# One level of seven block products for the output projections of two row tiles

## The chip, the cores and the metric

The kernel runs on one core of a Trainium2 chip. The metric is the device time of one execution in microseconds; the figure for a kernel is the median of its runs.

## What is computed

One decoder layer on 2048 rows of 1024 channels, in float32:

```python
hn = rms_norm(h, mix_pre_g)
proj = hn @ w_in                                   # q, k, v and the convolution's input u
attn_out = sliding_window_attention(q, k, v, attn_sinks, rel_bias)
conv_out = conformer_conv(u, conv_dw, conv_dw_b, conv_ln_g, conv_ln_b, w_conv_pw)
mixed = jnp.concatenate([attn_out, conv_out], axis=-1) @ w_out
h = h + rms_norm(mixed, mix_post_g)
hn = rms_norm(h, ffn_pre_g)
ff = (jax.nn.silu(hn @ w_gate) * (hn @ w_up)) @ w_down
h = h + rms_norm(ff, ffn_post_g)
```

The change concerns the line with `w_out`: 512 attention channels and 512 convolution channels times a 1024 x 1024 matrix. `w_join` is the convolution's pointwise matrix, multiplied beforehand into the lower half of `w_out`.

## The kernel before

**Tiles and precision.** The rows are cut into four tiles of 512 (numbered 0 to 3 in the code; "tiles 3 and 4" of the text are numbers 2 and 3). Each float32 operand is split into a high part (a rounded copy, made by ACT) and a low part (the rest, made by DVE), and a product takes three matmuls of 128x128 by 128x512: high by high, high by low, low by high.

**Stages.** The label behind the `@` in a tile's name tells the stage: `A` input projection, `B` attention, `C` convolution, `W` output projection and the norms behind it, `H` operands of the feed-forward, `F` gate and up projections, `G` down projection. The feed-forward works on two tiles at a time (first 0 and 1, then 2 and 3) and already uses one level of seven block products; its order for a pair is `stage_pre` (products that need the first tile of the pair alone), `stage_p1` and `stage_p2` (the down projection).

**Lanes.** The program is written out in one order. A main generator is run, and at each of its yields (a number, a nominal time) several lanes are pumped, each with its own rate, so that their instructions are emitted among the main ones. Instructions emitted earlier have priority; a compile-time pass then fixes the order on each engine, and each engine works strictly through its own. During `stage_p2` of the first pair (77 steps of 4 yields of 0.69), lane `lw` runs at rate 1.25 and holds the output projections of tiles 2 and 3.

**An output projection (`stage_w`).** For tiles 2 and 3 the four attention chunks are loaded from `mixT`, the four convolution chunks come from `stage_tail` within the same generator. Four steps of two chunks by two halves of the output: the weights are loaded (`raw`), their low parts are reloaded from `lo_out`, where the first tile's projection stored them, and `block_half` multiplies them for four row blocks in rotating PSUM banks `tr` and adds each result to `acc` (`mid@W`). The convolution's channels are needed only from the third step on. `norm_w` then makes the mean square, scales by the gains (`gb`), adds `x`, stores `h_scr`, norms again and stores `hn_scr`.

**What follows.** `stage_h_plain` reloads `hn_scr`, turns it on PE and makes the operands `B11` (tile `ql@H` in this pair) and `B21` (`mid@H`), each of four chunks, through tiles `gb`. `stage_pre` of the second pair begins with two products on `B11`, then two on `B21`. `B11.2` is queued in `lw`; `B21.2` in another lane, once the norm of tile 3 is emitted. `stage_h_sums` needs tile 3 too.

**Buffers.** Tiles of one name share a fixed count of buffers; those named below: `gb` 2, `ql` 4, `chl` 5, `mid` 4, `at` 2, `fc` 3, `yt` 1, `raw` 2, `w` 6. In PSUM: `mm` 4 banks, `tr` 3, `ct` 1.

**Taps.** The convolution of tiles 2 and 3 runs on DVE in lane `lc` (tile `y2`), ends in stores to `y_scr`, and `stage_tail` starts from there: load, turn on PE (L614), statistics, rsqrt, normalise, turn back (L667), swish.

Of the kernel before, what the change touches and what calls it, by code (L numbers as in the profile page):

```python
# [12 lines left out]
F32 = mybir.dt.float32  # L13
# [4 lines left out]
AF = mybir.ActivationFunctionType  # L18
ALU = mybir.AluOpType
# [4 lines left out]
D = 1024  # L24
DFF = 2816
P = 128
T = 512
NT = S // T
KC = D // P
# [8 lines left out]
def layer_kernel(ctx, tc, x, xT, cols, rows, sinks, relb, onehot, w_in, w_four, w_pw, w_out, w_gate, w_up, w_down, out):  # L38
    nc = tc.nc
# [61 lines left out]
    vtt = dve(nc.vector.tensor_tensor)  # L101
# [5 lines left out]
    def mat(*args, **kw):  # L107
        r = nc.tensor.matmul(*args, **kw)  # L108
        if not inlane[0]:
            lead_pe[0] = r  # L110
        return r
# [498 lines left out]
    def turner(yt, ycs):  # L610
        def turn(c):
            b = ct()
            for s in range(4):
                nc.tensor.transpose(b[:, s * P : (s + 1) * P], ycs[c][:, s * P : (s + 1) * P], ident)  # L614
            act(yt[:, :, c * P : (c + 1) * P], b.rearrange("p (s c) -> p s c", c=P), AF.Copy)

        return turn
# [16 lines left out]
    def stage_tail(t, sink=None):  # L634
        L = f"C{t}"
        lab[0] = L
        yt = t_("yt", (P, 4, 4 * P))
        ycs = []
        turn = turner(yt, ycs)
        for c in range(4):  # L640
            lab[0] = L
            y = f2("fc")
            nc.sync.dma_start(y, y_scr[c, :, t * T : (t + 1) * T])
            ycs.append(y)
            turn(c)
            yield 0.5
        yield from conv_tail(t, yt, sink)
# [111 lines left out]
    def ss(s):  # L759
        return slice((s % 4) * P, (s % 4 + 1) * P)  # L760
# [27 lines left out]
    def stage_w(w, spill, G, atag, htag, mtag, bank_of, norm=None):  # L788
        L = f"W{w}"
        lab[0] = L  # L790
        acc = [f4(atag) for _ in range(4)]

        def operand(m):
            a = hl(htag)
            act(a[:, 0], m, AF.Copy)
            vtt(a[:, 1], m, a[:, 0].bitcast(F32), ALU.subtract)
            return [a]

        def acts(gi, ms=None):
            return [operand(m) for m in ms or load(gi)]  # L800

        conv = []
        tail = stage_tail(w, lambda v: conv.append(operand(v))) if w > 1 else ()
        for y in tail:
            if y == YL2:
                break
            yield y
        lab[0] = L

        stage = spare_tile() if w == 1 else None  # L810

        def load(gi):
            ms = []
            pair_ = stage if w == 1 else t_("chl", (P, 2, T)) if w else t_("wx", (P, 2, T)) if gi == 0 else None
# [6 lines left out]
        gb = load_gb(0) if w > 1 else None  # L821
        if w != 1:
            yield 5.0 if w == 0 else 8.0
            lab[0] = L
        nxt = acts(0, first)
        for gi in range(KC // G):
            if w > 1 and G * gi == 4:
                yield from tail
                lab[0] = L
            aa = nxt if w < 2 or G * gi < 4 else conv[G * gi - 4 : G * gi - 4 + G]  # L830
            for n in range(2):
                lab[0] = L
                more = gi + 1 < KC // G and (w < 2 or G * gi + G < 4)
                if n == 0 and more:
                    if w < 2 and G * gi + G == 4:
# [9 lines left out]
        last = norm_w(w, spill, acc, mtag, gb)  # L845
        if norm:
            norm(last)
        else:
            yield from last

    def norm_w(w, spill, acc, mtag, gb):
# [12 lines left out]
        for s in range(4):  # L864
            lab[0] = L
            post_scale(acc[s], gb, r[:, s : s + 1])
            r0 = w * T + s * P
            if s == (2 if mtag == "fa" else 0):
                xt = f4("wx")
                nc.sync.dma_start(xt, x[r0 : r0 + P])  # L870
                vtt(acc[s], xt, acc[s], ALU.add)
            else:
                for n in range(2):
                    cs = slice(n * T, (n + 1) * T)
                    xt = f2(mtag if s == 1 or w > 1 else "fa")
                    nc.sync.dma_start(xt, x[r0 : r0 + P, cs])
                    vtt(acc[s][:, cs], xt, acc[s][:, cs], ALU.add)
            nc.sync.dma_start(h_scr[r0 : r0 + P], acc[s])
            act(junk, acc[s], AF.Square, accum_out=ssq2[:, s : s + 1])
            yield 5.0  # L880
        lab[0] = L
        r2 = rsqrt(ssq2, 4, D, False)
        yield 3
        lab[0] = L
        for s in range(4):
            act(acc[s], acc[s], AF.Copy, scale=r2[:, s : s + 1])
        if spill:
            yield 2.0
            lab[0] = L
            for s in range(4):  # L890
                r0 = w * T + s * P
                nc.sync.dma_start(hn_scr[r0 : r0 + P], acc[s])
        yield 0.1
        hns[w] = acc
# [8 lines left out]
    def split_f(x, w):  # L903
        act(w[:, 0], x, AF.Copy)  # L904
# [497 lines left out]
    def since(lane, name, dt):  # L1402
        return name in lane.done and clk[0] >= lane.done[name] + dt
# [51 lines left out]
    RC0, RC1, RC2, RC3, RW0, RW, RB, LC = 0.7, 1.1, 0.35, 0.9, 1.7, 1.25, 0.8, 100  # L1455
# [3 lines left out]
    CS = 10  # L1459
    YC = 3  # L1460
    YP = 1.5
    YL, YL2 = 12, 20
# [12 lines left out]
    lc = Lane(RC0, LC)  # L1475
    lw = Lane(RW0, 0)
# [7 lines left out]
    lw.rates = {"W0": RW0, "C2": RW, "W2": RW, "C3": RW, "W3": RW}  # L1484

    def run(gen):
        for c in gen:
# [65 lines left out]
    ws, ops = (0, 1), {}  # L1553
    for n, off in (("B11", 0), ("B21", 4)):
# [85 lines left out]
```

## Time and profile before

| | us |
|---|---|
| median of 3 runs | 1907.33 |
| lowest, highest | 1906.63, 1907.36 |
| span of the profiled execution | 1907.9 |
| PE busy | 1889.1 |
| DVE busy | 1490.7 |
| ACT busy | 970.6 |
| first matmul of the first pair's down projection | 950.8 |
| first matmul of the second pair's feed-forward | 1265.5 |

The page gives no time of the profiled execution beside its span; the span is 0.6 us above the median. PE is TensorE, DVE VectorE, ACT ScalarE, POOL GpSimd, SP SyncE; SPq and ACTq are DMA issues by SP and ACT. A row of a group reads: line, engine, operation, output<-inputs, shapes, count | busy us, mean ns of one | idle us before it and what ended that. A row of a window reads: its bounds and length, then busy us and instructions of PE, weight loads, DVE, ACT and POOL (of one tile's instructions alone where the window is of a tile, with the engines that it has), PE's granted clock, the DMA engines' busy share and GB/s. A row of the timeline reads: start, length, engine, line, operation, count and, in brackets, the idle time before. A row of the chain of waits reads: start, length, what.

### The profile page before, as it was taken

The page shows a single profiled execution, that of the slowest core. Times are in us where ns is not written, and L with a number is a line of the kernel's source. Part 1 is how long each engine was busy: PE and PEld are TensorE (multiplying, and loading weights), DVE is VectorE, ACT ScalarE, POOL GpSimd, SP SyncE. Part 2 cuts the span into 40 slices and gives each one's busy share as a digit, 9 for nine tenths or more (in the row PEclk, how much of TensorE's full clock was granted, in tenths as well). Part 3 has the DMA queues.
Part 4 walks back from the last instruction along what each step waited for, and adds up shares of the span by engine and source line. Part 5 has one row for each costly group of instructions (what it writes and reads, how often), then busy time and mean ns, then how long its engine had stood idle before and what let it go on. Part 6 is the DMA issues. An engine that isn't in the chain of part 4 may idle for free.

```text
span 1907.9 us, 26569 instructions
## 1 busy us (share of the span) xinstructions
PE 1889.1 (99%) x8714; PEld 1530.1 (80%) x8714; DVE 1490.7 (78%) x2721; ACT 970.6 (51%) x1912; POOL 179.2 (9%) x196
## 2 busy tenths in 40 slices
PE   9999999999999999999999999999999999999998
PEld 8777777777777888888888878788888888888886
DVE  6999999987966999999996765887567674455558
ACT  5356445566667433433445574685443433345452
POOL 2010001110000000000000000010033233211002
PEclk9999999999999999999999999999999999999999
DMA  9887746679688677877776596798554443375663
GB/s 353 300 281 238 248 160 207 230 228 318 218 274 276 232 234 232 293 261 243 244 268 195 196 326 212 259 333 307 166 176 156 160 138 127 116 258 187 206 220 133
DMA packets 226491, 439.29 MB, mean 230 GB/s; under 512 B 22536, under 2 KB 48560, under 8 KB 226352
## 3 DMA queue, kind: packets, MB, share of 16 engines
q1 hardware_dynamic: 207344, 411.37, 64.8%
q10 hardware_dynamic: 17088, 19.93, 2.9%
q0 software_dynamic: 1920, 6.29, 0.9%
q8 instruction: 68, 1.11, 0.2%
q14 instruction: 71, 0.58, 0.1%
HBM read 318.48 MB, written 119.02 MB: 229 GB/s over the span
## 4 chain that ended last, share of the span: by engine, by line
PE 78%; DVE 9%; DMA 8%; ACT 3%; issue 2%; SPq 0%; ACTq 0%; DVEq 0%; POOL 0%; POOLq 0%
PE mm@F L108 34%; PE mm@G L108 16%; PE mm@A L108 14%; PE tr@W L108 5%; PE mm@W L108 3%; PE tr@B L108 2%; PE ct@J L108 1%; DVE w@F L85 1%; DVE mid@W L85 1%; DMA hl@A<-x 1%; DVE sm@G L85 1%; DVE y2@C L85 1%; DMA chl@H<-hT 1%; DVE hl@G L85 1%; DMA chl@F<-w_gate 1%
## 5 line engine op out<-in xcount | busy, mean ns | idle before, releaser
L108 PE MATMUL mm@F<-hl@H,w@F 128*128 128x512 f32 x1056 | 255.8, 391 | 1.8 <-ACT mm@F L1058 1.6
L108 PEld LDWEIGHTS mm@F<-hl@H,w@F 128*128 128x128 f32 x1056 | 197.7, 188 | 44.8 <-ACT mm@F L1058 2.8
L108 PE MATMUL mm@G<-hl@G,hl@G 128*128 128x512 f32 x924 | 226.1, 393 | 2.3 <-ACT hl@G L904 1.5
L904 ACT ACTIVATE w@F<-chl@F 128x512 fp32r<-128x512 f32 x220 | 136.5, 626 | 170.2 <-PE mm@F L108 158.7
L108 PEld LDWEIGHTS mm@G<-hl@G,hl@G 128*128 128x128 f32 x924 | 171.5, 188 | 39.7 <-ACT hl@G L904 2.2
L108 PE MATMUL mm@G<-w@G,hl@G 128*128 128x512 f32 x876 | 199.8, 389 | 0.6 <-DVE w@G L85 0.6
L108 PEld LDWEIGHTS mm@G<-w@G,hl@G 128*128 128x128 f32 x876 | 164.3, 188 | 35.2 <-DVE w@G L85 1.0
L108 PE MATMUL mm@A<-hl@A,w@A 128*128 128x512 f32 x792 | 192.2, 394 | 0.0
L108 PEld LDWEIGHTS mm@A<-hl@A,w@A 128*128 128x128 f32 x792 | 146.8, 188 | 32.5 <-issue 1.7
L85 DVE TENSOR_TENSOR w@F<-chl@F,w@F 128x512 fp32r<-128x512 f32 x198 | 148.1, 753 | 25.5 <-ACT w@F L904 25.0
L85 DVE SCALAR_TENSOR_TENSOR y2@C<-g2@C,colt,y2@C 128x1024 f32<-128x1024 f32 x120 | 154.0, 1283 | 0.2
L108 PE MATMUL mm@F<-mid@H,w@F 128*128 128x512 f32 x528 | 130.6, 390 | 1.0 <-DVE w@F L85 0.9
L108 PE MATMUL mm@F<-ql@H,w@F 128*128 128x512 f32 x528 | 129.7, 390 | 0.2
L108 PE MATMUL mm@F<-p@H,w@F 128*128 128x512 f32 x528 | 129.1, 389 | 0.0
L108 PE MATMUL mm@F<-x@H,w@F 128*128 128x512 f32 x528 | 127.8, 390 | 0.0
L108 PEld LDWEIGHTS mm@F<-mid@H,w@F 128*128 128x128 f32 x528 | 98.8, 188 | 22.2 <-DVE w@F L85 1.3
L108 PEld LDWEIGHTS mm@F<-ql@H,w@F 128*128 128x128 f32 x528 | 98.7, 188 | 21.3 <-DVE w@F L85 0.6
L108 PEld LDWEIGHTS mm@F<-x@H,w@F 128*128 128x128 f32 x528 | 98.7, 188 | 21.3 <-issue 0.8
L108 PEld LDWEIGHTS mm@F<-p@H,w@F 128*128 128x128 f32 x528 | 99.1, 188 | 20.6
L133 ACT ACTIVATE w@A<-raw@A 128x512 fp32r<-128x512 f32 x100 | 60.9, 625 | 80.2 <-PE mm@A L108 46.3
L85 DVE TENSOR_TENSOR w@G<-raw@G,w@G 128x512 fp32r<-128x512 f32 x72 | 50.2, 698 | 64.2 <-ACT w@G L904 63.4
L108 PE MATMUL mm@W<-w@W,hl@W 128*128 128x512 f32 x384 | 97.1, 399 | 0.8 <-DVE x@W L85 0.4
(322 smaller groups left out, 3363.9 us busy)
## 6 DMA issues: line engine op xcount, KB each, us to landing
mids<-fa@F SPq DMA_DIRECT2D x154, 256.0 KB, 3.3
raw@A<-w_in SPq DMA_DIRECT2D x50, 512.0 KB, 4.9
w@A<-lo_in SPq DMA_DIRECT2D x84, 256.0 KB, 4.0
fa@G<-mids SPq DMA_DIRECT2D x74, 256.0 KB, 4.7
fc@G<-mids SPq DMA_DIRECT2D x72, 256.0 KB, 3.5
w@W<-lo_out SPq DMA_DIRECT2D x48, 256.0 KB, 4.8
chl@F<-w_gate SPq DMA_DIRECT2D x22, 512.0 KB, 4.4
raw@F<-w_gate SPq DMA_DIRECT2D x22, 512.0 KB, 4.2
```

The costliest lines, as they stand in the source:

```text
L85: r = op(*args, **kw)
L108: r = nc.tensor.matmul(*args, **kw)
L133: act(w[:, 0], raw, AF.Copy)
L904: act(w[:, 0], x, AF.Copy)
```

## The change

The projections of tiles 2 and 3 are taken out of `stage_w` and made together by one level of seven block products: the two tiles and the two halves of the channels (attention, convolution) form 2 x 2 blocks on the left, the two halves of the channels and of the outputs 2 x 2 blocks of the weights. `stage_vsums` makes four sums of row blocks and four of weight blocks and stores them in DRAM (`vs0`, `vs1`). `stage_v` makes the seven kinds in turn, each over four chunks and in four PSUM banks held throughout (`tr` three times, `ct`), with results kept in the two tiles' `acc` (`mid` and `chl`). It loads all its operands, splits both sides itself and no longer reads `lo_out`. `stage_tail` of both tiles now stores its channels to `mixT`. Lane `lw` holds, in this order: both tails, the sums, the products, both norms (with one pair of gain tiles), `B11.2`. The loop of `stage_w` remains for tiles 0 and 1.

```diff
@@ stage_w
-        conv = []
-        tail = stage_tail(w, lambda v: conv.append(operand(v))) if w > 1 else ()
-        for y in tail:
-            if y == YL2:
-                break
-            yield y
...
+    def stage_vsums(ws, ma, mb_):
+        L = f"W{ws[0]}"
+        cols_ = [slice(w * T, (w + 1) * T) for w in ws]
+
+        def load(c):
+            lab[0] = L
+            a = [t_("chl", (P, 2, T)) for _ in range(2)]
+            b = [t_("raw", (P, 2, T)) for _ in range(2)]
+            for j in range(2):
+                nc.sync.dma_start(b[j], (w_join if j else w_out)[c].rearrange("p (a b) -> p a b", a=2))
+                nc.sync.dma_start(a[j], mixT[c::4, :, cols_[j]].rearrange("j p t -> p j t"))
+            return a, b
+
+        yield 6.0
+        nxt = load(0)
+        yield 6.0
+        for c in range(4):
+            a, b = nxt
+            (a11, a12), (a21, a22) = [(t[:, 0], t[:, 1]) for t in a]
+            (b11, b12), (b21, b22) = [(t[:, 0], t[:, 1]) for t in b]
+            for to, o, p_, op, q_, dst in (
+                (0, b11, b12, ALU.subtract, b11, mb_), (2, b12, b22, ALU.subtract, b12, mb_),
+                (1, b22, b22, ALU.subtract, b11, mb_), (3, b21, b21, ALU.subtract, b22, mb_),
+                (2, a22, a21, ALU.add, a22, ma), (1, a21, a11, ALU.subtract, a21, ma),
+                (0, a11, a22, ALU.subtract, a11, ma), (3, a12, a12, ALU.subtract, a11, ma)):
+                lab[0] = L
+                vtt(o, p_, q_, op)
+                nc.sync.dma_start(dst[to, c], o)
+                yield 0.8
+            if c < 3:
+                nxt = load(c + 1)
+                yield 2.0
+
+    def stage_v(ws, ma, mb_, accs, gbs):
+        L = f"W{ws[0]}"
+        lab[0] = L
+        banks = [tr(), tr(), tr(), ct()]
+        for acc, tag in zip(accs, ("mid", "chl")):
+            acc += [f4(tag) for _ in range(4)]
...
+        stage = t_("yt", (P, 2, 2, T))
+        steps = [(ty, c) for ty in range(7) for c in range(4)]
...
+        def load(h):
+            if 2 * h < len(steps):
+                lab[0] = L
+                rb = t_("raw", (P, 2, T))
+                nc.sync.dma_start(rb, right(*steps[2 * h]).rearrange("j p t -> p j t"))
+                ra = stage[:, h % 2]
+                nc.sync.dma_start(ra, left(*steps[2 * h]).rearrange("j p t -> p j t"))
...
+        def split(i):
+            if i < len(steps):
+                lab[0] = L
+                b = split_f(rawb[i], hl("w"))
+                lo(rawb.pop(i), b, False)
+                a = split_f(rawa[i], hl("ql"))
+                lo(rawa.pop(i), a, False)
+                opsd[i] = a, b
+
+        def after(ty, b):
...
+            if ty == 0:
+                act(u1, o, AF.Copy)
+            elif ty == 1:
+                nc.vector.tensor_copy(c11, o)
+                act(o, u1, AF.Copy)
+            elif ty == 2:
+                act(u2, o, AF.Copy)
+            elif ty == 3:
+                vtt(c22, o, u2, ALU.subtract)
+            elif ty == 4:
+                nc.vector.tensor_copy(c21, o)
+                act(o, u2, AF.Copy)
+            elif ty == 5:
+                vtt(c22, c22, o, ALU.add)
+            else:
+                act(c12, o, AF.Copy)
...
+        for i, (ty, c) in enumerate(steps):
+            split(i + 3)
+            if i % 2 == 0:
+                load(i // 2 + 3)
...
+            for b in range(4):
...
+                for z, (p_, q_) in enumerate(((ah, w[:, 0]), (ah, w[:, 1]), (al, w[:, 0]))):
+                    mat(banks[b], p_, q_, start=i == 0 and z == 0, stop=c == 3 and z == 2, skip_group_check=True)
+                if c == 3:
+                    after(ty, b)
+                yield 0.69
...
@@ the order
-    lw.add("W2", stage_w(2, True, 2, "mid", "ql", "at", tr), lambda: since(lc, "T2", CS))
-    lw.add("W3", stage_w(3, True, 2, "mid", "ql", "at", tr, norm=lambda g: lw.add("N3", g)),
-           lambda: since(lc, "T2", CS))
+    for w in ws:
+        lw.add(f"C{w}", stage_tail(w), lambda: since(lc, "T2", CS))
+    vs = [dr.tile([4, 4, P, T], F32, name=f"vs{i}") for i in range(2)]
+    accs, gbv = ([], []), []
+    lw.add("WS", stage_vsums(ws, *vs))
+    lw.add("V", stage_v(ws, *vs, accs, gbv))
+    for w in ws:
+        lw.add(f"N{w}", norm_w(w, True, accs[w - 2], "at", gbv))
     lw.add("B11.2", stage_h_plain(ws, ops, "B11", 0))
```

More of the change, by code (lines that the diff above doesn't have):

```diff
@@ L813, in load @@
             ms = []
-            pair_ = stage if w == 1 else t_("chl", (P, 2, T)) if w else t_("wx", (P, 2, T)) if gi == 0 else None
+            pair_ = stage if w else t_("wx", (P, 2, T)) if gi == 0 else None
             for c in range(G * gi, G * gi + G):
@@ L820, in stage_w @@
         first = load(0)
-        gb = load_gb(0) if w > 1 else None
-        if w != 1:
-            yield 5.0 if w == 0 else 8.0
+        if w == 0:
+            yield 5.0
             lab[0] = L
@@ L826, in stage_w @@
         for gi in range(KC // G):
[L827 to L830, printed above, removed]
+            aa = nxt
             for n in range(2):
                 lab[0] = L
-                more = gi + 1 < KC // G and (w < 2 or G * gi + G < 4)
+                more = gi + 1 < KC // G
                 if n == 0 and more:
-                    if w < 2 and G * gi + G == 4:
+                    if G * gi + G == 4:
                         ld.until(f"C{w}")
@@ L844, in stage_w @@
                 yield from block_half(acc, list(zip(aa, ws)), n, gi == 0, L, bank_of)
-        last = norm_w(w, spill, acc, mtag, gb)
+        last = norm_w(w, spill, acc, mtag)
         if norm:
@@ L849, in stage_w @@
             yield from last
-    def norm_w(w, spill, acc, mtag, gb):
+    def stage_vsums(ws, ma, mb_):
[28 more added lines that the diff above has]
+                yield 2.0
@@ new lines, in stage_v, with left, right @@
+    def stage_v(ws, ma, mb_, accs, gbs):
[4 more added lines that the diff above has]
+            acc += [f4(tag) for _ in range(4)]
+        n0, n1 = slice(0, T), slice(T, D)
+        cols_ = [slice(w * T, (w + 1) * T) for w in ws]
+        stage = t_("yt", (P, 2, 2, T))
+        steps = [(ty, c) for ty in range(7) for c in range(4)]
+        rawa, rawb, opsd = {}, {}, {}
+        def left(ty, c):
+            if ty < 2:
+                return mixT[4 * ty + c : 4 * ty + c + 2, :, cols_[0]]
+            if ty == 4:
+                return mixT[4 + c : 6 + c, :, cols_[1]]
+            return ma[{2: 0, 3: 1, 5: 2, 6: 3}[ty], c : c + 2]
+        def right(ty, c):
+            if ty in (0, 1, 6):
+                return (w_join if ty else w_out)[c : c + 2, :, n1 if ty == 6 else n0]
+            return mb_[{2: 1, 3: 2, 4: 3, 5: 0}[ty], c : c + 2]
+        def load(h):
[5 more added lines that the diff above has]
+                nc.sync.dma_start(ra, left(*steps[2 * h]).rearrange("j p t -> p j t"))
+                for j in range(2):
+                    rawa[2 * h + j], rawb[2 * h + j] = ra[:, j], rb[:, j]
+        def split(i):
[7 more added lines that the diff above has]
+        def after(ty, b):
+            lab[0] = L
+            o = banks[b]
+            (c11, c12), (c21, c22) = [(acc[b][:, n0], acc[b][:, n1]) for acc in accs]
+            u1, u2 = c21, c12
+            if ty == 0:
[14 more added lines that the diff above has]
+                act(c12, o, AF.Copy)
+        load(0)
+        load(1)
+        yield 8.0
+        for i in range(3):
+            split(i)
+        load(2)
+        yield 2.0
+        for i, (ty, c) in enumerate(steps):
+            split(i + 3)
+            if i % 2 == 0:
+                load(i // 2 + 3)
+            if i == len(steps) - 4:
+                lab[0] = L
+                gbs += load_gb(0)
+            for b in range(4):
+                lab[0] = L
+                (a, w) = opsd[i]
+                ah, al = a[:, 0, ss(b)], a[:, 1, ss(b)]
+                for z, (p_, q_) in enumerate(((ah, w[:, 0]), (ah, w[:, 1]), (al, w[:, 0]))):
[3 more added lines that the diff above has]
+                yield 0.69
+            del opsd[i]
@@ L852, in norm_w @@
+    def norm_w(w, spill, acc, mtag, gb=None):
         L = f"W{w}"
@@ L1483, in layer_kernel @@
     lc.rates = {"T0": RC0, "T1": RC1, "T2": RC2}
-    lw.rates = {"W0": RW0, "C2": RW, "W2": RW, "C3": RW, "W3": RW}
+    lw.rates = {"W0": RW0, "C2": RW}
     def run(gen):
```

1 line of the change is left out of this document (removed).

## The prediction

> **What bounds the kernel now.** I read the page first, then the groups of instructions, then the chain of waits and the timelines from 930 to 1300 us, where the changed stage lies.
>
> ```profile
> span 1907.9 us, 26569 instructions
> PE 1889.1 (99%) x8714; PEld 1530.1 (80%) x8714; DVE 1490.7 (78%) x2721; ACT 970.6 (51%) x1912; POOL 179.2 (9%) x196
> ```
> ```profile
> L108 PE MATMUL mm@G<-hl@G,hl@G 128*128 128x512 f32 x924 | 226.1, 393 | 2.3 <-ACT hl@G L904 1.5 <-DVE p@G L1297 0.6
> ...
> L108 PE MATMUL tr@W<-w@W,ql@W 128*128 128x512 f32 x192 | 51.2, 391 | 0.0
> ...
> L108 PE MATMUL tr@W<-w@W,ql@C 128*128 128x512 f32 x192 | 47.7, 392 | 0.0
> ```
>
> PE works all the time, so a product that goes is time that goes, as long as PE still has something ready. The projections of tiles 3 and 4 are the 192 + 192 matmuls into `tr@W`; they run among the 924 of the first down projection (`mm@G`). The next rows show the pace of PE with nothing else in the way, the load of the stage, and where the chain of waits leaves it.
>
> ```profile
> 1000.22 14.52 PE mm@G L108 x64
> ...
> 1256.45 6.18 DMA hn_scr<-mid@W
> 1263.07 6.64 DMA at@H<-hn_scr
> ```
> ```profile
> 944.00:1260.00 316.00, 313.69 (x1420) 257.48 (x1419) 236.69 (x423) 187.13 (x332) 3.72 (x12) 1.00 0.75 252
> 950.00:1087.00 137.00, 137.00 (x626) 113.04 (x625) 105.77 (x168) 73.15 (x128) 0.00 (x0) 1.00 0.71 235
> ```
>
> 64 matmuls in 14.52 us are 0.227 us each. In the stretch of 316 us PE stood idle 2.3 us and DVE was busy 75%. At its end PE is still full, but the chain already runs through the stored norm of tile 4 (`hn_scr`) and its reload: the projections and their norms end hardly before the next stage needs them.
>
> **The change, part by part.**
>
> *Products.* Two tiles took 2 x 8 x 2 x 4 x 3 = 384 matmuls; seven kinds by 4 chunks by 4 banks by 3 are 336. 48 x 0.227 = 10.9 us of PE go. This is the whole gain; no other engine or wait on the path is relieved.
>
> *DVE, ACT.* Out go 16 operand splits and 48 additions on DVE, and 64 copies on ACT (32 weights, 16 operands, 16 first blocks). In come 56 splits, 16 evacuations and 32 sums on DVE, and 56 + 20 copies on ACT: 40 more on DVE and 12 more on ACT, by the rows below 27.5 us and 7.5 us. Over the whole stage that is 264 us of DVE, which fits; where it falls comes below.
>
> ```profile
> L904 ACT ACTIVATE hl@G<-mb@G 128x512 fp32r<-128x512 f32 x77 | 48.2, 625 | 68.9 <-PE mm@G L108 59.8 <-DMA mb@G<-td 6.3 <-issue 2.2
> ...
> L85 DVE TENSOR_TENSOR wx@G<-wx@G 128x512 f32<-128x512 f32 x11 | 7.6, 687 | 4.0 <-DMA wx@G<-w_down 4.0
> ```
>
> *Order of the lane.* This is where I expect the time to turn. Before, the first half of a projection (attention rows) needed no convolution result, and PE ran it from 951 us while DVE was still busy with the taps. After, one lane holds both tails, the sums, all products, both norms and then `B11.2`. Its yields come to 259 units; at rate 1.25 that is 207.7 of the 212.5 units of the down projection (before: 150.4). So even the order as written has no slack left, and the lane also waits for data:
>
> ```profile
> 1004.67 0.33 SPq L631 DMA_DIRECT2D y_scr<-y2@C  x1
> ```
> ```profile
> 1014.58 0.60 PE L614 MATMUL ct@C<-ident,fc@C 128*128 128x128 f32 x4
> 1033.18 0.27 PE L667 MATMUL ct@C<-ident,yt@C 128*128 128x128 f32 x1
> ...
> 1037.11 0.60 PE L667 MATMUL ct@C<-ident,yt@C 128*128 128x128 f32 x4
> ...
> 1052.12 0.60 PE L667 MATMUL ct@C<-ident,yt@C 128*128 128x128 f32 x4
> ```
>
> The last taps are stored at 1004.7; tile 3's tail turns back at 1033.2, and its four chunks take 3.9 us each at the pace of the first two (15.7 us; 18.9 us as they were). There is one `yt` buffer, so tile 4's tail follows: statistics 18.6 us (1014.6 to 1033.2), chunks 15.7 us. `yt` is free at 1033.2 + 15.7 + 18.6 + 15.7 = 1083. The product stage keeps its rows in `yt` too, so its first load starts there, not where the order of the lane puts it. With a load and a split (6.5 and 1.3 us):
>
> ```profile
> raw@W<-w_out SPq DMA_DIRECT2D x6, 512.0 KB, 6.5
> ...
> hn_scr<-mid@W SPq DMA_DIRECT2D x8, 512.0 KB, 5.4
> ...
> at@H<-hn_scr SPq DMA_DIRECT2D x4, 256.0 KB, 5.5
> ```
>
> its first matmul comes at about 1091. Bounds: 1079 with chunks of 2.4 us (the two ACT reads and the turn alone), 1097 with both tails' chunks as before's. The sums lie within this time on DVE and do not push it: weights first, and kinds 1 and 2 need none.
>
> *Length of the products.* 336 x 0.227 = 76.2 us if PE did nothing else. Before, the projection's share of PE was
>
> ```profile
> 1150.00:1200.00 50.00, 32.89 (x134) 24.77 (x132) 15.10 (x22) 0.00 (x0) 1.00 0.59 183
> ```
>
> 134 of 220 slots, 61%. The new stage waits for a bank only at the end of a kind, so more: I take 75%, 102 us, between 61% (125 us) and 95% (80 us). The products end at 1193 (1159 to 1222). PE loses nothing here: the down projection fills in.
>
> *Norms, now behind everything.* Before, tile 3's norm ran at 1081 to 1137 beside tile 4's products. After, both stand behind the last product, and `B11.2` behind both.
>
> ```profile
> 1080.61 0.69 DVE L85 TENSOR_TENSOR mid@W<-mid@W,tr@W 128x512 f32<-128x512 f32 x1 [2.17 <-PE tr@W L108]
> ...
> 1226.19 0.68 DVE L85 TENSOR_TENSOR ql@H<-gb@H,ql@H 128x512 fp32r<-128x512 f32 x1
> ...
> 1266.61 0.69 DVE L85 TENSOR_TENSOR mid@H<-gb@H,mid@H 128x512 fp32r<-128x512 f32 x1
> ```
> ```profile
> 1129.14 2.94 SPq L892 DMA_DIRECT2D hn_scr<-mid@W  x3
> ```
> ```profile
> 1210.50 0.67 ACT L942 ACTIVATE gb@H<-tr@H,colt 128x512 f32<-128x512 f32 x1
> ...
> 1228.43 0.69 ACT L942 ACTIVATE gb@H<-tr@H,colt 128x512 f32<-128x512 f32 x1 [1.41 <-DMA hT<-gb@H]
> ```
>
> From the last addition to the last store's issue 51.5 us (1080.6 to 1132.1); landing 5.4; reload 5.5; the four operands of `B11.2` 16.4 us (1210.5 to 1226.9): 79 us. `B11.2` is complete at 1193 + 79 = 1272.
>
> *Where PE runs dry.* The down projection ended at 1265.5; less 10.9 us, PE has nothing more after 1254.6, and the next feed-forward cannot begin without `B11.2`.
>
> ```profile
> 1265.49 3.04 PE L108 MATMUL mm@F<-ql@H,w@F 128*128 128x512 f32 x12
> ...
> 1273.41 1.87 PE L108 MATMUL mm@F<-mid@H,w@F 128*128 128x512 f32 x7
> ```
>
> It begins 6 us later than before (1272 for 1265.5), after an idle 17 us. Its third product needs `B21.2`, which comes through the same two `gb` buffers: at the earliest 16.4 us after `B11.2`, at the latest the 38.9 us that it took (1228.4 to 1267.3). I take 16.4, since it then has DVE and ACT almost to itself: 1288, where before had 1273.4. That is +14.6 us, or +37 by the other end. Tile 4's norm is needed only after the 32 products that use tile 3 alone (32 x 12 x 0.227 = 87 us later) and stays hidden.
>
> *Traffic.* Out: 16 pairs of weights and 32 stored low halves (0.52 and 0.26 MB each) and 8 rows, 18.9 MB. In: 16 loads and 32 stores of the sums, 28 loads of the products, 8 stored rows, 33.6 MB. Up to 1087 the stretch moved 235 GB/s x 137 us = 32.2 MB; without some ten weight steps (10.5), with 19 more steps of the down projection (10.0), the sums (16.8) and rows (2.1) it is 50.6 MB, 369 GB/s. The 19 steps: PE has some 585 slots there beside the turns, and the down projection had 355 of them (first row below); 230 more, by 12. The best 10 us of this trace is the second row:
>
> ```profile
> 950.00:1087.00 137.00, 89.08 (x355) 66.24 (x356) 4.01 (x6) 3.55 (x6) 1.00 0.71 235
> ```
> ```profile
> 1220.00:1230.00 10.00, 10.00 (x46) 8.29 (x45) 6.29 (x10) 7.72 (x14) 0.00 (x0) 1.00 1.04 388
> ```
>
> So it just fits, and I price it at nothing; were it 10 us too slow, the products would start 10 us later. The Trainium skill, page "DMA: Bandwidth & Descriptors", section "Bandwidth", says that transfers between HBM and SBUF are held to about 358 GB/s per core; the row of 388 GB/s differs and decides. By the page the sums would take 141 us instead of 137, an estimate, and the forecast would be 4 us higher.
>
> **Sum.** 1907.9 us is the span of the profiled execution, 0.6 us above the median of 1907.3. 1907.9 + 14.6 - 0.6 = 1922 us. PE's clock reads 1.00 in every row above, and PE's gaps come to 2.3 us in all there. The Trainium skill, page "TensorE: Matmul & The Clock Gate", section "Part 1: The HAM clock gate", says that an idle window of about 3.4 us halves PE's clock until about as long a busy one; no run here shows it, and by it the two gaps would add some 3 us, an estimate.
>
> **The rivals.**
>
> *All of the gain arrives.* The same chain decides: if the products end by 1167 instead of 1193, `B21.2` is there (95 us later) when PE wants it, and the time is 1907.3 - 10.9 = 1896.4. Between 1167 and 1178 a part of it arrives; at 1178 nothing is won or lost. For it: the first matmul at 1079 with a share of 87% gives this, and with the lane late its instructions stand ahead of the down projection's in the order. Against: the share was 61%, and tails, `yt` and norms must all go at their best. 25% for a time over 0.2% below before; 0.2%, 3.8 us, is about what a measurement of this kernel tells from no change.
>
> *The sums fill DVE as well.* Before 1087, DVE was busy 105.8 us of 137.
>
> ```profile
> 950.00:1087.00 137.00, 16.09 (x24) 9.13 (x16) 1.00 0.71 235
> ```
>
> Take off the additions (16.1) and 12 operand splits (8.2); add 32 sums (22.0), 38 splits of the down projection, which alone feeds PE (26.1), and tile 4's tail (10): 139.6 of 137. The waits of before, 31 us, do not all vanish; with a third of them left the products start 10 us later, and PE lacks splits in the meantime. 1922 + 10 = 1932, up to 1945 with the 38.9 us of `B21.2` in part. For it: DVE serves strictly in order. Against: PE was full at 944 to 1000 us with DVE nearly so. 20%.
>
> *It cancels.* The products end near 1178: within 0.2%. 8%.
>
> **How the numbers follow.** The forecast, norms exposed behind the last product, has 47%: 1922, by its bounds 1911 to 1940. Slower in all is 0.67 with the second rival, faster 0.25, same 0.08. The range goes from 1899, where most of the faster case is still inside, to 1944.
>
> **What would show it.** In the changed profile: 336 matmuls of the new stage, first near 1091, last near 1193; no PE work between about 1255 and 1272; a second gap before the products that read `mid@H`; that idle time put down to `ql@H`, `mid@H` or to loads of `hn_scr`. Wrong if the products end before 1170, if `B11.2` is complete before the down projection ends, or if PE stands idle mainly earlier, on `hl@G`.

## Result and profile after

| | us |
|---|---|
| before, median of 4 runs | 1907.18 (1906.63 to 1907.36) |
| after, median of 4 runs | 1988.62 (1987.55 to 1990.02) |
| ratio | 1.043 (95% interval 1.0415 to 1.044) |

The change makes the kernel 81 us slower; the forecast was 1922, in a range to 1944. The profiled execution took 1989.33 us. Its page, totals and the rows by slices of a fortieth of the span:

```profile
span 1987.6 us, 26591 instructions
PE 1892.1 (95%) x8666; PEld 1529.8 (77%) x8666; DVE 1516.0 (76%) x2761; ACT 978.5 (49%) x1924; POOL 174.8 (9%) x196
...
PE   9999999999999999999989999429999999999998
...
PEclk9999999999999999999999999759999999999999
```

The counts are those that the prediction worked out: 48 matmuls fewer, 40 instructions more on DVE, 12 more on ACT. Yet PE is busy 3 us longer: the 10.9 us that were saved came back as matmuls that took longer, at a lower granted clock or one by one between waits, and on top of it PE stands idle. One shallow dent is at slice 21, one deep hole at slices 26 and 27. The same two stretches as windows, first of before and then of after:

```profile
950.00:1050.00 100.00, 100.00 (x454) 82.64 (x453) 80.92 (x124) 50.20 (x87) 0.00 (x0) 1.00 0.71 236
1250.00:1350.00 100.00, 99.17 (x455) 81.54 (x454) 76.97 (x148) 66.90 (x128) 6.36 (x23) 1.00 0.90 306
```
```profile
950.00:1050.00 100.00, 90.51 (x378) 73.23 (x377) 85.78 (x118) 41.66 (x74) 0.00 (x0) 0.93 0.78 255
1250.00:1350.00 100.00, 30.93 (x119) 23.08 (x118) 59.64 (x147) 55.11 (x105) 6.85 (x24) 0.62 0.60 205
...
1270.00:1300.00 30.00, 0.00 (x0) 0.00 (x0) 14.45 (x39) 10.13 (x17) 0.00 (x0) 0.50 0.45 151
```

76 matmuls too few in the first stretch and 336 in the second; at the prediction's 0.227 us that is 93.5 us of PE, and less the 10.9 us of saved matmuls 82.6, the whole loss (81). So the late hole holds four fifths of it (turns on PE count as matmuls in these rows, so this is rough). What stands in it is the tail of the chain that the prediction feared: the operands of `B11.2` (`ql@H`) come late, because the norms come late, because the products come late (timeline rows):

```profile
1170.92 2.20 PE L108 MATMUL tr@W<-w@W,ql@W 128*128 128x512 f32 x9
...
1263.35 0.84 PE L108 MATMUL ct@W<-w@W,ql@W 128*128 128x512 f32 x3
...
1307.91 1.09 PE L1033 MATMUL tr@H<-ident,fc@H 128*128 128x128 f32 x4 [43.71 <-DMA fc@H<-hn_scr]
...
1312.69 0.79 PE L108 MATMUL mm@F<-ql@H,w@F 128*128 128x512 f32 x1 [3.69 <-ACT ql@H L1056]
...
1327.00 1.11 PE L1033 MATMUL tr@H<-ident,at@H 128*128 128x128 f32 x4 [11.30 <-DMA at@H<-hn_scr]
```

The block products run from 1171 to 1264; PE then waits 43.7 us for tile 3's stored norm and 11.3 us for more chunks of it. The down projection had ended by then, its last matmul at 1230.3. The single `mm@F` at 1312.7 takes 0.79 us, twice the 0.39 us of a matmul at full clock.

### The profile page after: what moved, and what is told of

Same layout as the page of the kernel before. It is cut to its first block, busy times and chain, and to the rows that moved or that the text cites. A ratio compares the mean times of both kernels' runs of the same rounds, so it can differ in the third digit from the quotient of the medians.

```text
span 1987.6 us, 26591 instructions
## 1 busy us (share of the span) xinstructions
PE 1892.1 (95%) x8666; PEld 1529.8 (77%) x8666; DVE 1516.0 (76%) x2761; ACT 978.5 (49%) x1924; POOL 174.8 (9%) x196
## 3 DMA queue, kind: packets, MB, share of 16 engines
q8 instruction: 68, 1.11, 0.2%
## 4 chain that ended last, share of the span: by engine, by line
PE 65%; DVE 15%; DMA 12%; issue 3%; ACT 3%; SPq 1%; POOL 0%; DVEq 0%; ACTq 0%; POOLq 0%
PE mm@F L108 25%; PE mm@G L108 15%; PE mm@A L108 14%; PE tr@W L108 3%; DVE y2@C L85 2%; PE mm@W L108 2%; PE tr@B L108 2%; DVE w@F L85 2%; DMA mids<-fa@F 1%; DMA vs<-raw@W 1%; PE ct@J L108 1%; DVE chl@F L85 1%; DVE fa@F L85 1%; DMA mb@G<-w_down 1%; DVE hl@G L85 1%
## 5 line engine op out<-in xcount | busy, mean ns | idle before, releaser
L108 PE MATMUL mm@G<-hl@G,hl@G 128*128 128x512 f32 x924 | 222.2, 399 | 10.9 <-ACT mm@G L1432 5.0
L108 PEld LDWEIGHTS mm@G<-hl@G,hl@G 128*128 128x128 f32 x924 | 175.5, 192 | 49.7 <-ACT mm@G L1432 5.4
L85 DVE TENSOR_TENSOR w@F<-chl@F,w@F 128x512 fp32r<-128x512 f32 x198 | 146.2, 744 | 27.3 <-ACT w@F L1015 26.9
L108 PE MATMUL mm@F<-ql@H,w@F 128*128 128x512 f32 x528 | 135.0, 400 | 13.3 <-ACT ql@H L1056 10.2
```

What stands on the lines that cost most here:

```text
L85: r = op(*args, **kw)
```

## Experiments

The theory after the result: the time is set by the end of the last block product, and this end is late because (a) the weight sums delay the taps, (b) the conv tails, now ahead of all products, follow each other slowly, (c) the row sums follow the tails. Rivals: the lane's new order alone; the pace at which the lane is written out; norms that stand in a bad order. Each kernel ran once, beside the kernel before (1906.6 to 1909.4 us there); the four runs of after lie 2.5 us apart, so a difference of 2 or 3 us says nothing. e2, e3, e8 and e12 leave out operands of the layer and serve for their time alone. The times in the last columns are the start of the last store of the taps, and of the first and last matmul of the products.

| run | what differs from after | us | taps stored | products |
|---|---|---|---|---|
| after | | 1989.3 | 1041.1 | 1170.9 to 1263.8 |
| e1 | plain projections, new order | 1914.5 | 1004.0 | 949.7 to 1215.1 |
| e2 | products ahead of tails | 1942.7 | 1027.2 | 1023.8 to 1149.2 |
| e3 | no weight sums | 1967.0 | 1018.2 | 1136.6 to 1247.5 |
| e4 | weight sums on GpSimd | 1981.9 | 1024.7 | 1152.7 to 1262.4 |
| e5 | `B11.2` ahead of tile 4's norm | 1990.7 | 1039.5 | 1169.6 to 1262.4 |
| e6 | e4, lane 2.4 times as fast | 1988.5 | 1029.1 | 1157.5 to 1267.0 |
| e7 | e4, `B11.2` and `B21.2` ahead of that norm | 1989.5 | 1026.4 | 1154.5 to 1264.1 |
| e8 | e2 and e3 | 1928.3 | 1048.1 | 967.0 to 1123.3 |
| e9 | weight sums 300 us earlier | 1981.0 | 1031.1 | 1155.0 to 1261.3 |
| e10 | e9, tails' turns in three banks | 1969.8 | 1034.9 | 1127.0 to 1249.3 |
| e11 | e10, own buffers for tile 4's tail | 1973.7 | 1024.6 | 1128.0 to 1253.2 |
| e12 | no sums at all, three banks | 1936.2 | 1016.5 | 1106.3 to 1204.7 |

**The order alone (e1).** Two plain projections by `stage_w` with all their weights and first halves, but in the new order: both tails first, their rows stored to `mixT` and reloaded.

```diff
-    lw.add("WS", stage_vsums(ws, *vs))
-    lw.add("V", stage_v(ws, *vs, accs, gbv))
+    lw.add("W2", stage_w(2, True, 2, "mid", "ql", "at", tr))
+    lw.add("W3", stage_w(3, True, 2, "mid", "ql", "at", tr, norm=lambda g: lw.add("N3", g)))
```

> The lane's new order alone: both tails first, their rows stored, then the two projections of eight chunks as before with stored low halves of the weights, no sums and no block products. If the loss comes from the order (products that may begin only when both tails are through), most of the 81 us stays: 1950 to 1985 us, first matmul of the projections after 1090 us, a gap of PE before the second pair's feed-forward of 40 us or more. If the block products and their sums are the cause, the time is within 15 us of before, 1900 to 1922 us.

It lost only 5 us to the kernel before that ran beside it. The attention half has its data early, so its matmuls begin at 949.7 though they are written behind the tails. The lane's order as such is not the cause. What sets after apart is that none of its products begins before the tails are through. This isn't a need of all of them: the first kind multiplies attention rows of tile 3 by plain weights, as e1's early matmuls do. But its rows go through `yt`, which the tails hold, as the prediction said (see e12 and e11 below).

**Products that need no tail (e2, e8).** Attention rows stand in for convolution rows, and the tails follow the products. In e8 the products also read plain weight blocks, and no weight sums are made.

```diff
-                nc.sync.dma_start(a[j], mixT[c::4, :, cols_[j]].rearrange("j p t -> p j t"))
+                nc.sync.dma_start(a[j], mixT[min(c, 2) : min(c, 2) + 2, :, cols_[j]].rearrange("j p t -> p j t"))
...
     lw.add("V", stage_v(ws, *vs, accs, gbv))
+    for w in ws:
+        lw.add(f"C{w}", stage_tail(w), lambda: since(lc, "T2", CS))
```

> The sums and the seven kinds are made ahead of the tails and read attention rows where they should read convolution rows, so that they wait for no tap; the tails run behind them for nothing. All work is still done. If the wait for the tails is the cause, the gap of PE before the second feed-forward goes and the 10.9 us of 48 matmuls arrive: 1895 to 1905 us. If the norms behind the last product, or DVE's and the DMA engines' load, are the cause by themselves, 1930 us or more.

> The products do not need the conv tails (attention rows stand in for convolution rows; tails come after the products) and there are no weight sums (plain weight blocks are read); row sums, seven products and norms stay. Theory: tails ahead of the products plus weight sums beside the taps are the whole cause; without either no gap of TensorE at 950 to 1050, the products end before 1130 and the time is 1895 to 1910 (1907 less the 11 us of saved matmuls, plus a few). Rival: seven products in a row beside the down projection, or two norms in one go behind them, cost by themselves: 1920 or more.

Neither reached the 1895 to 1910 that the cure should give, so both are only half an answer. In e2 the products still waited, to 1023.8, for the `raw` buffers that the weight sums held. Without the weight sums (e8) they began at 967.0 and ended at 1123.3, and 14.5 us went. But the tails now lie between the products and the norms, and `hn_scr` was stored as late as 1212 to 1268 us, so PE ran dry at 1250 to 1300 all the same:

```profile
1250.00:1300.00 50.00, 32.06 (x137) 23.54 (x136) 34.98 (x95) 41.76 (x82) 6.87 (x24) 0.76 0.87 299
```

These two runs replace one serial chain by another and don't price the tails. In e8 the products do begin early, with neither data nor buffers to wait for from a tail.

**Weight sums: left out (e3), on another engine (e4), at another time (e9).** e3 reads plain weight blocks in their place. e4 makes them on GpSimd behind the down projection's own sums, e9 on GpSimd in the first half of the first feed-forward. The first two lines of the cut go in all three, the next two are the new sums of e4 and e9, the last two their place in e9.

```diff
-                (0, b11, b12, ALU.subtract, b11, mb_), (2, b12, b22, ALU.subtract, b12, mb_),
-                (1, b22, b22, ALU.subtract, b11, mb_), (3, b21, b21, ALU.subtract, b22, mb_),
...
+                ptt(o, p_, q_, ALU.subtract)
+                nc.sync.dma_start(mb_[to, c], o)
...
+    lt.add("TB", stage_wsums(vs[1]))
     run(stage_pre(ws, ops, mids[0], keeps[0]))
```

> The four weight sums are left out: 16 DVE sums, their 8 loads and 16 stores go, and the kinds that should read them read plain blocks of the output weights. The taps ended at 1041 us after and at 1005 before. If the weight sums (on DVE, and their stores in SP's queue) delay the taps, the taps end by 1015 and the time falls by 25 to 40 us, to 1950 to 1963. If it is the down projection's own splits, now twice as dense beside the taps, the taps still end after 1030 and the time falls by less than 12 us, to 1977 or more.

> The sixteen weight sums are made early, on GpSimd behind the down projection's own sums, and the row-sum stage makes row sums alone. If the weight sums cost through their 16 VectorE subtractions and 24 transfers among the taps' (950 to 1006 us), the time falls to that of the kernel without weight sums: 1962 to 1972 us, last tap store near 1018, no gap of TensorE between 960 and 1040. If it is the traffic as such that costs, whenever it is, 1980 to 1990.

> The weight sums are made on GpSimd some 300 us earlier still, in the first half of the first feed-forward, so that neither their loads, nor their subtractions, nor their stores lie near 900 to 1010 us. Theory 'beside the taps': the sums cost only because they stand beside the taps and the start of the down projection; 1960 to 1970 us, as without sums (1967), last tap store near 1018, no gap of TensorE at 950 to 1050. Rival 'traffic wherever it is': 1978 or more.

Without them the early dent is gone (first row, e3), the taps are stored 23 us earlier and the time falls by 22. Moved to GpSimd at nearly the same time, only 7 us come back and the dent stays (e4): so it isn't DVE's 16 subtractions alone. Moved 300 us earlier, the dent at 950 is gone too (e9), but PE loses about as much where they now lie: 129.6 us busy of 140 at 520 to 660, where after has 139.6. Windows of e3, of e4, of e9 and of after:

```profile
950.00:1050.00 100.00, 99.77 (x448) 82.19 (x447) 85.69 (x133) 48.34 (x86) 0.00 (x0) 1.00 0.67 216
```
```profile
950.00:1000.00 50.00, 39.83 (x163) 30.59 (x162) 49.55 (x55) 15.87 (x29) 13.83 (x8) 0.93 0.86 285
```
```profile
520.00:660.00 140.00, 129.59 (x589) 103.16 (x588) 98.17 (x168) 85.03 (x164) 26.34 (x20) 0.98 0.85 296
950.00:1050.00 100.00, 99.77 (x446) 82.26 (x446) 92.26 (x134) 48.40 (x87) 0.00 (x0) 1.00 0.70 227
```
```profile
520.00:660.00 140.00, 139.62 (x644) 112.26 (x643) 103.06 (x190) 91.62 (x178) 2.84 (x4) 1.00 0.77 259
```

So both theories of e9 hold in part: the sums cost 22 us in after's place and 14 (1981.0 less 1967.0) in the first feed-forward. Of these 14, 11.6 us are there before the changed stage begins: the down projection's first matmul comes at 960.3 in e9 and at 948.7 in e3. What they cost through in after stands in its chain of waits between 950 and 1012:

```profile
950.28 0.61 DVE raw@W L85
950.91 4.71 DMA vs<-raw@W
955.67 1.28 DVE y2@C L85
...
961.18 5.30 DMA vs<-raw@W
...
983.83 6.83 DMA vs<-raw@W
990.68 4.82 DMA raw@W<-w_join
995.59 0.70 DVE raw@W L85
...
1006.35 5.36 DMA vs<-raw@W
```

A subtraction, its store, the reload of the buffer, and taps and splits queued on DVE between them: the store and the reload are on the path, and the prediction counted only their bytes.

**The pace of the lane (e6).**

```diff
-    lw.rates = {"W0": RW0, "C2": RW}
+    lw.rates = {"W0": RW0, "C2": 3.0, "V": RW}
```

> As the kernel with early weight sums, and the lane that places the conv tails, the row sums and the head of the products among the down projection's steps runs 2.4 times as fast (3.0 for 1.25) up to the first block product, then at 1.25 as before. Theory 'pace': the written pace and not the data sets when the products begin; their first matmul moves from about 1137 to 1105 to 1115 us and the time falls by 20 to 30, to 1937 to 1948. Theory 'data': tails and sums wait for stores and loads; first product within 5 us of 1137, time within 5 of the kernel with early weight sums.

The text took e3's start (1137) for that of e4 (1152.7), which wasn't known then. Beside e4 the products began 5 us later, not earlier, and the time rose by 6.5 us. The written pace is not what holds them back.

**The banks and buffers of the tails (e10, e11).** The first change below is in both runs, the second in e11 alone.

```diff
-            b = ct()
+            b = tr() if t > 1 else ct()
...
-        yt = t_("yt", (P, 4, 4 * P))
+        yt = [t_("raw", (P, 2, T)) for _ in range(2)] if t == 3 else t_("yt", (P, 4, 4 * P))
```

> As the run with the sums 300 us earlier, and the turns of the two conv tails go through the three banks of the products (idle until these begin) and not through the one bank that they share. Theory 'one bank': the single bank spaces a tail's chunks at 6.4 us; with three, both tails end 20 us or more earlier and the time falls by as much. Rival 'order on the engines': a chunk stands 6.4 us behind the one before because of what is queued between them; first product and time within 6 us of the run with the sums 300 us earlier.

> As the run with three banks for the turns, and the tail of tile 4 works in two buffers of its own (those of the raw weights) instead of waiting for the one yt buffer, so the two tails can lie beside each other. Theory 'tails in line': the products start late because tile 4's tail waits for tile 3's buffer; their first matmul comes 30 to 50 us earlier than in the run with the sums 300 us earlier, the gap after the last product shrinks by the same, 1920 to 1940 us. Rival: the tails are spaced by the engines' order anyway, within 8 us of the run with three banks.

e10 beside e9, turns back (L667) of tile 4, timelines of e9 and then of e10:

```profile
1118.47 0.60 PE L667 MATMUL ct@C<-ident,yt@C 128*128 128x128 f32 x4
1126.65 0.60 PE L667 MATMUL ct@C<-ident,yt@C 128*128 128x128 f32 x4
1130.32 0.60 PE L667 MATMUL ct@C<-ident,yt@C 128*128 128x128 f32 x4
1141.25 0.60 PE L667 MATMUL ct@C<-ident,yt@C 128*128 128x128 f32 x4
```
```profile
1106.14 1.47 PE L667 MATMUL tr@C<-ident,yt@C 128*128 128x128 f32 x12
1115.42 0.60 PE L667 MATMUL tr@C<-ident,yt@C 128*128 128x128 f32 x4
```

With three banks, three chunks go in one row, and the products begin 28 us earlier: the single bank does space the chunks. It isn't the bank's own cycle alone, though. In after the two ACT reads of the chunk turned at 1134.75 end at 1137.60, and the next turn comes at 1142.70, behind 33 matmuls of the down projection that stand before it in PE's order. That the compile-time pass put them there because of the bank is argued, not shown. The products end only 12 us earlier than in e9, and the time falls by 11, so half of theory 'one bank' held. They now take 122 us for 106. Two waits of 6.1 us in all, in which the first kind's results had to wait until stores of row sums freed `chl`, show the row sums at work (the last of these stores came at 1167.4); the rest of the 16 us isn't explained.

e11 came within 4 us of e10, as its rival said. It didn't bring the overlap that it was made for: tile 4's first turn came at 1081.1 (1079.7 in e10), its first load from `y_scr` was issued at 1074.8 only, 13 us behind tile 3's last turn back. These loads share the three `fc` buffers with tile 3's chunks, which would explain it, but no run gave them others. Whether two overlapping tails would help stays open. e11 shows something else: `yt` was free behind tile 3's tail, and the first kind's rows were loaded from 1062.0 on. But now tile 4's tail held `raw`; the first weights were requested at 1118.1, 1 us after its last turn, and the first product, which waited for them, came at 1128.0. One shared buffer took the place of the other.

**The order behind the products (e5, e7).** Tile 4's norm goes behind `B11.2`. In e7, which starts from e4, it goes behind `B21.2` as well (the line with `B21.2` is e7's alone), and the next feed-forward's sums are held until that norm is emitted.

```diff
-    for w in ws:
-        lw.add(f"N{w}", norm_w(w, True, accs[w - 2], "at", gbv))
+    lw.add("N2", norm_w(2, True, accs[0], "at", gbv))
     lw.add("B11.2", stage_h_plain(ws, ops, "B11", 0))
+    lw.add("B21.2", stage_h_plain(ws, ops, "B21", 4))
+    lw.add("N3", norm_w(3, True, accs[1], "at"))
```

> In the lane, the operands of the second feed-forward's first products stand between the two norms instead of behind both, and tile 4's norm loads its own gains. After, the first operand's rows were loaded at 1305 us but the other buffer's only at 1323, behind tile 4's rows of x. If the second norm in front is what makes the last stretch long, these operands are complete some 20 us earlier and the time is 1965 to 1973 us. If the first norm's own chain sets it, within 6 us of 1988.6.

> As the kernel with early weight sums, and both first operands of the second feed-forward (all eight turned chunks of tile 3) are made before tile 4's norm. Theory 'norms in line': what TensorE waits for after the last block product is two norms and two sets of chunks one behind the other; with one norm ahead instead of two the gap shrinks by 20 to 28 us: 1938 to 1948. Rival: as when only the first set was moved (1990.7 beside 1988.6), the wait goes over to the transfers that stand ahead in the queue: within 6 us of the kernel with early weight sums.

Both theories fell: e5 came within 2 us of after, and e7 was 8 us slower than e4, which it starts from. e7 did what it should at first: `mm@F` starts at 1312.5 and PE is 88% busy at 1300 to 1400. Then it stands for 20 us of the next 40 (windows of e7):

```profile
1300.00:1400.00 100.00, 88.43 (x380) 71.69 (x381) 59.02 (x137) 63.90 (x126) 9.93 (x24) 0.90 0.90 312
1400.00:1440.00 40.00, 19.63 (x85) 14.97 (x84) 36.61 (x58) 21.40 (x38) 2.85 (x1) 0.70 0.75 258
```

The 32 products that use tile 3 alone are some 87 us of PE; tile 4's norm, stored at 1371 to 1376 instead of 1334 to 1337 in e4, and the sums on it (`stage_h_sums`) weren't there when they were used up. Tile 3's result is complete only with the last kind and tile 4's with the one before, so nearly all the work behind the products has one length, and the order of the norms only chooses where PE waits. No run changed the order of the kinds, in which tile 3, the one needed first, comes last.

**No sums (e12).** The products read plain blocks of weights and of rows; tails, seven kinds, norms as in after, turns in three banks.

> Neither weight sums nor row sums are made (the products read plain blocks of weights and rows in their place), the tails' turns go through the three banks of the products, and everything else stays: tails ahead of the products, seven kinds, norms after them. Over the runs so far the time was the end of the last block product plus 720 to 725 us. Theory 'row sums gate': after the tails the products wait for 16 row sums that go through the store; without them they follow the tails directly, begin near 1112 and end at 1205 to 1225, so the time is 1926 to 1946. Rival 'the products' own pace': they end 11 us earlier than in the run without weight sums, as the three banks gave there, near 1238, time 1955 to 1960. In either case the line of +721 should hold.

```profile
L108 PE MATMUL tr@W<-w@W,ql@W x252: 387/389/504, 1170.9 to 1263.1; 128*128 128x512 f32 x126
```
```profile
L108 PE MATMUL tr@W<-w@W,ql@W x252: 389/389/389, 1106.3 to 1204.0; 128*128 128x512 f32 x126
```

(The group of the first three banks' products, of after and of e12: lengths in ns, first and last start.) The time is 52 us lower than after's, 1936.2, in the range of theory 'row sums gate'; the products begin 65 us earlier and end 59 earlier. But the theory had the place wrong. The first product follows the tails' last store by 4 us here, and by 2 us in e10 with all its row sums. Counted from the down projection's first matmul (965.9 in e10, 947.7 in e12), the products begin 2.5 us earlier than in e10 and end 26 us earlier. By this estimate (e10 also has the weight sums, made long before) the row sums cost in the products' length, not at their start. What the start waits for is `yt`: the first load of rows is issued at 1097.2, as soon as tile 4's last turn (1096.6) has read the buffer, though these attention rows were there long before. Even without sums the kernel is 27 us slower than the kernel before beside it: the tails end before the products begin, and the norms follow the products. No run gave the products buffers that no tail holds, so what that would be worth stays open. The line from products to time held to within 11 us. From the last product to the end of the execution it is 719.5 to 721.5 us in e3, e4, e6, e9, e10 and e11, 725 to 728 in after, e5 and e7, and 731.5 in e12.

## Why the prediction was wrong

*Direction and chain: right.* Slower had 0.67, by the mechanism named: norms exposed behind the last product, `B11.2` late, PE dry. From the prediction's own figures, end of products 1193 gives 1922, a distance of 729. Measured are 725 in after and 731.5 in e12, and e12, whose products end at 1205 (12 us behind the forecast's 1193), takes 1936, 14 us over the forecast. That the distance fits is in part luck, as the norm chain below shows.

*Step that failed: the start of the products*, 1091 forecast, 1170.9 measured. Term by term, 79.9 us late:

| term | forecast | measured | late by |
|---|---|---|---|
| taps stored | 1004.7 | 1041.1 | 36.4 |
| tile 3 to its first turn back | 28.5 | 28.8 | 0.3 |
| its chunks, to tile 4's first turn | 15.7 | 28.7 | 13.0 |
| tile 4's statistics, to its turn back | 18.6 | 36.2 | 17.6 |
| its chunks, to the first product | 23.5 | 36.2 | 12.7 |

The rows of the middle three, from after's timeline:

```profile
1069.85 0.27 PE L667 MATMUL ct@C<-ident,yt@C 128*128 128x128 f32 x1
...
1091.07 0.60 PE L667 MATMUL ct@C<-ident,yt@C 128*128 128x128 f32 x4
1098.59 0.60 PE L614 MATMUL ct@C<-ident,fc@C 128*128 128x128 f32 x4
...
1115.67 0.60 PE L614 MATMUL ct@C<-ident,fc@C 128*128 128x128 f32 x4
1134.75 0.60 PE L667 MATMUL ct@C<-ident,yt@C 128*128 128x128 f32 x4
```

- *Taps.* The forecast left them where they were. 23 us of the 36 are the weight sums (e3). The other 13 come neither with the weight sums nor with the order: they remain in e12 (1016.5) and are absent in e1 (1004.0). Between 950 and 1015 the down projection alone feeds PE and has 270 matmuls in e3, 220 in e1 and 170 before, each twelve with two low halves on DVE. That this is the cause is argued, not shown.
- *Tails.* The forecast took the pace of tile 3's first two chunks, 3.9 us, for turns that share one bank; after has them 5.5 to 8.5 us apart. With three banks the span from the taps' store to the first product was 92 us in e10 and 90 in e12, against 86 forecast; with one it was 124 in e9, 118 in e3 and 130 in after.
- *Sums.* "The sums lie within this time on DVE and do not push it" was the wrong sentence. Weight sums: 22 us (e3). The row sums cost as well, but behind the first product: e12 beside e10, 26 us at the products' end once the later start of e10's down projection is taken off.
- *Traffic.* Priced at nothing, because 369 GB/s fits under 388. Over the stretch the bandwidth indeed wasn't the limit: the stage moved 255 GB/s at 950 to 1050. The chain of waits shows single stores and reloads. For moments the DMA engines were full all the same: at 980 to 990, where PE's wait of 4.1 us lies, their busy share was 1.00 at 340 GB/s, for 0.45 and 142 GB/s in the same 10 us of before. So a share of crowding in these waits isn't ruled out. The Trainium skill's limit of 358 GB/s (page "DMA: Bandwidth & Descriptors", section "Bandwidth") didn't bind either: after moved 382 GB/s at 1350 to 1360.

*Length of the products*: 92.9 us for 102, within the forecast's 80 to 125, but for the last 33 us of it the down projection had run out, so the share of 75% wasn't put to the test. *Norm chain*: from the last product at 1264 to the last split of `ql@H` at 1345 it took 81 us for 79. This is luck, for two errors cancel: up to the issue of the norm's last store it was 38 us for 51.5, and from there, with landing, reload and the four operands, 43 for 27.3. *Second operand*: at least 16.4 us behind `B11.2`; the last split of `mid@H` came 12.5 us behind it, at 1357.7, a little less than the 16.4 that the text took for the least. *Down projection*: dry at 1254.6 forecast, ended at 1231; with the products late it ran ahead alone, and then the products alone filled 33 us.

*Sums of the text.* With its own latest end of the products, 1222, the chain gives 1951 us, more than the 1940 of its bounds and the 1944 of its range; 259 units at rate 1.25 are 207.2, not 207.7, on which nothing hangs.

*Rivals.* "The sums fill DVE as well" had the right place and 20%, but a price of 10 us where the weight sums alone put 23 on the taps; it also put it on DVE alone, and e4 shows that moving the subtractions to GpSimd returns only 7. "All of the gain arrives" would have needed products that end by 1167; even without any sums they end at 1205. The sign that the text gave for a wrong forecast, PE idle mainly earlier and on `hl@G`, came true in small part: 9.5 us idle at 950 to 1050, of which 9.1 are put down to ACT's copies at the banks (`mm@G`, `p@G`).

## What to carry to other kernels

A level of block products over two tiles can't finish before the last operand of either tile is there, and here it completes the tile that is needed first at its very end. Before counting saved matmuls, find the last operand and the first user, and add up the chain between them: here 48 matmuls (11 us) were saved, and the next stage's first operand was complete 80 us after the time at which before began that stage. When steps that stood among other work come to stand in a row, neither the old trace's gaps nor the bare cycle of their shared bank gives their pace: here the gaps said 3.9 us, the bank was free again after 2.1 to 5.2 us, and 5.5 to 8.5 us came. Ask of the first product which buffers it needs and who holds them last, not only when its data is there. Sums that go through DRAM can put a store and a reload on the path, beside their bytes and subtractions.

## What the hardware showed

PE's granted clock fell to 0.50 within the idle stretch after the products and stayed there until PE had steady work again (rows of after):

```profile
1270.00:1280.00 10.00, 0.00 (x0) 0.00 (x0) 9.02 (x23) 0.96 (x3) 0.00 (x0) 0.50 0.00 0
...
1320.00:1330.00 10.00, 1.97 (x8) 1.57 (x8) 7.22 (x19) 3.32 (x9) 5.11 (x16) 0.50 0.63 188
...
1350.00:1360.00 10.00, 9.37 (x42) 6.87 (x41) 6.41 (x20) 5.31 (x10) 0.00 (x0) 1.00 1.06 382
```

Single waits of 4.1 and 5.0 us did it too: the clock averages 0.79 at 990 to 1000 and 0.75 at 1020 to 1030. The Trainium skill, page "TensorE: Matmul & The Clock Gate", section "Part 1: The HAM clock gate", says that an idle window of about 3.4 us halves the clock and a busy one of that length restores it; by that rule the trace agrees, with 0.50 and a matmul of 0.79 us. What it cost isn't separated by any run. At 990 to 1000 PE got through 36 matmuls where before has 46, and behind the products the turns on the chain took 1.05 to 1.11 us for 0.60.
